# Skip weights loaded as rows, 512-column passes for v and half the output projection, a gelu of four steps, and two gather tiles of one bank

## The chip, the cores and the metric

The kernel runs on one core of a Trainium2 chip. The metric is the device time of one execution in microseconds (us). Before the change three runs gave 1151.94, 1154.35 and 1153.66 us, median 1153.66.

Five engines work side by side and meet at semaphores: TensorE (PE, matmuls; its weight loads are PEld), VectorE (DVE), ScalarE (ACT), GpSimd (POOL) and SyncE (SP, which here only issues DMAs). Sixteen DMA engines move all data for the core.

## What is computed

One layer of a hybrid backbone on 512 latent tokens and 256 context tokens, 1024 channels. After an RMSNorm with modulation comes one wide input projection, and from it two branches: a bidirectional Mamba-2 scan with skip weights per head (d_skip), and a gMLP branch whose halves u and v go through a gelu (v also through a layernorm). Gated, summed and projected by w_o they are added to the input h. Then follows an expert-choice mixture: 16 experts, each takes its best 64 of the 512 tokens.

```python
y = y + d_skip.astype(xh.dtype)[:, None] * xh
u, v = jnp.split(jax.nn.gelu(uv), 2, axis=-1)
sgu = spatial_gating(u, v, n_chunks, ln_w, ln_b, w_s, b_s)
merged = jax.nn.sigmoid(gate_a) * (ssd @ w_pa) + jax.nn.sigmoid(gate_b) * (sgu @ w_pb)
h = h + g1 * (merged @ w_o)
gate, idx = lax.top_k(softmax(xf @ router_w), 64)
hid = silu(xf[idx] @ w_gate) * (xf[idx] @ w_up)
h = h + g2 * scatter(idx, (hid @ w_down) * gate)
```

## The kernel before, in words

All tiles have 128 partitions. The projections of the first half (lines 272 to 965) run each product as three matmuls: an operand is split into a rounded part and its rest (`split`, lines 72 to 78: ACT casts the weights to `wh`, DVE subtracts to get `wl`), and hi times hi, hi times lo and lo times hi are added in one PSUM bank. A scheduler puts the instructions of each engine in an order of its own; on the engine they then run strictly in that order, and each waits for the tiles that it reads and for the readers of the tile that it overwrites. The unit of those waits is the tile, not the part of it that is touched.

**Start (lines 81 to 310).** SP loads x (4 pieces of 512 KB), the first modulation weights `aw`, the first input weights `w0` and the context tokens `ct`, in that order. POOL issues small loads on a queue of its own: rows of parameters, `alog` (one row for all 128 partitions, line 124), `dtb`, and `dsk`, the skip weights (lines 128 to 130): partition 64s+i gets the eight elements s, s+2, s+4, ... The first large matmuls (`gemv`, line 237) wait for `aw`. Then PE transposes x (line 255) and the context (line 261), and ACT copies the results out.

**v (lines 583 to 638).** `token_major` takes the weights in four column blocks of 256. A 1 MB piece of weights is split in two halves, and each half gives 48 matmuls (4 token tiles, 4 rows of k, 3 products) of 256 columns. At the end of a block each token tile goes through `gelu2` (lines 608 to 614: two ACT and three DVE steps) and, every second block, through bn_stats (line 623). The four accumulators `acc` of a block are the only ones, so the next block's first matmul on a token tile waits until its gelu has read the old one out. The steps of the last scan group are laid between (`steps(scans, 2)`). After the last block DVE finishes the layernorm (lines 631 to 636); only then do the pools of this part close, and a load of w_s into the place that they leave (line 751) can go. The u projection (line 770) starts meanwhile.

**Output projection (lines 913 to 965).** The same `token_major` with w_o. A block's token tile goes through `residual` (lines 916 to 921: two DVE steps and one ACT step through the single tile `t0`, so one after the other). `logits` (line 925) transposes two 128-column pieces of h and multiplies by the router's weights, and needs all four token tiles of the block.

**Experts (lines 966 to 1225).** DVE finds the best 64 tokens of each expert (lines 1029 to 1039). The experts go in eight pairs; `project` (line 1089) multiplies the gathered tokens by w_gate and w_up, `down` (line 1154) by w_down, each weight being used once. `piece` (line 687) hands out the 1 MB weight tiles and asks for the next ones: about twenty tiles form a ring, and a load into one waits until PE has read it. The gather of the next pair's tokens is `channels` (line 1074): 16 times 4 matmuls in two halves, each half followed by four ACT steps that scale it into `xg`. Both halves write one PSUM tile of two banks (lines 1106 and 1144). The last pair is cut finer, and the rows go out at line 1238.

Of the kernel before, what the change touches and what calls it, by code (L numbers as in the profile page):

```python
# [7 lines left out]
F32 = mybir.dt.float32  # L8
# [4 lines left out]
AF = mybir.ActivationFunctionType  # L13
OP = mybir.AluOpType
# [3 lines left out]
GELU_C = 0.7978845608028654  # L18
GELU_K = 0.044715

NT = 4
NK = 8
# [11 lines left out]
def tile_backbone(  # L34
# [18 lines left out]
    W = w_in.rearrange("l k n -> (l k) n")  # L53
# [7 lines left out]
    sp = es_s.enter_context(tc.tile_pool(name="sp", bufs=2))  # L61
# [7 lines left out]
    def wtile():  # L69
        return wp.tile([128, 2048], F32, name="w")  # L70
# [5 lines left out]
    def wsplit(hi, lo, src, lo_eng=None):  # L76
        with tc.high_priority():
            split(hi, lo, src, lo_eng)
# [47 lines left out]
    G.memset(dtb, 0.0)  # L126
    nc.gpsimd.dma_start(dtb[0:32, :], dram(dt_bias, 0, [[1, 32], [1, 1]]))
    dsk = sp.tile([128, NK], F32, bufs=1)
    for s in range(2):
        nc.gpsimd.dma_start(dsk[64 * s:64 * s + 64, :], dram(d_skip, s, [[0, 64], [2, NK]]))  # L130

    def rsqrt(o, v, scr, n):

# [30 lines left out]
    def acc():  # L164
        return ps.tile([128, 512], F32, name="acc")
# [4 lines left out]
    with tc.tile_pool(name="st", bufs=2) as st:  # L170
# [81 lines left out]
        for kt in range(NK):  # L252
            p = aux()
# [3 lines left out]
        for k2 in range(NK // 2):  # L257
            p = aux()
# [6 lines left out]
        xmh = xmp.tile([128, NK, 512], F32R, name="xmh")  # L265
        xml = xmp.tile([128, NK, 512], F32R, name="xml")
# [85 lines left out]
    def hl_tile(a, b):  # L352
        return [hl.tile([128, 1024], F32R, name=n)[:, :a * b].rearrange("p (a b) -> p a b", a=a) for n in ("wh", "wl")]
# [8 lines left out]
    def w_cols(src, c0, n):  # L362
        return dram(src, c0, [[src.shape[1], 128], [128 * src.shape[1], NK], [1, n]])
# [7 lines left out]
    for o, n, parts in ((0, 512, (xT,)), (512, 256, (xch.bitcast(F32), xcl.bitcast(F32)))):  # L371
        p = acc()[:, :n]
# [185 lines left out]
    def ahead(gen):  # L558

        cur = next(gen)  # L560
        for n in gen:
            yield cur
            cur = n
        yield cur
# [15 lines left out]
            scans = ssd_group(g)  # L580


    def token_major(src, n0, lh, ll, evac, wt=lambda nb: wtile()):

        def weights():
            for nb in range(4):
                w = wt(nb).rearrange("p (k n) -> p k n", k=NK)
                load(w, w_cols(src, n0 + 256 * nb, 256))
                for kh in range(2):
                    wh, wl = hl_tile(4, 256)  # L590
                    wsplit(wh, wl, w[:, 4 * kh:4 * kh + 4, :])
                    yield nb, kh, wh, wl

        for nb, kh, wh, wl in ahead(weights()):
            if kh == 0:
                pp = [acc()[:, :256] for _ in range(NT)]
            for t in range(NT):
                for k in range(4):
                    kt = 4 * kh + k
                    a = slice(128 * t, 128 * t + 128)  # L600
                    T.matmul(pp[t], lh[:, kt, a], wh[:, k, :], start=kt == 0, stop=False)  # L601
                    T.matmul(pp[t], ll[:, kt, a], wh[:, k, :], start=False, stop=False)  # L602
                    T.matmul(pp[t], lh[:, kt, a], wl[:, k, :], start=False, stop=kt == NK - 1)  # L603
                if kh == 1:
                    evac(nb, t, pp[t])
            yield

    def gelu2(o, p, a):

        S.activation(a, p, AF.Square)  # L610
        V.tensor_scalar(a, a, GELU_C * GELU_K, GELU_C, op0=OP.mult, op1=OP.add)
        V.tensor_mul(a, a, p)
        S.activation(o, a, AF.Tanh)
        V.scalar_tensor_tensor(o, o, 1.0, p, op0=OP.add, op1=OP.mult)  # L614

    vt = big.tile([128, NT, 1024], F32, name="F")
    bn = sp.tile([128, NT, 2, 6], F32, bufs=1)

    def v_out(nb, t, p):
        a = sp.tile([128, 512], F32, name="tm")[:, :256]  # L620
        gelu2(vt[:, t, 256 * nb:256 * nb + 256], p, a)
        if nb % 2:
            V.bn_stats(bn[:, t, nb // 2, :], vt[:, t, 256 * nb - 256:256 * nb + 256])

    for _ in token_major(W, 4128, xmh, xml, v_out):
        steps(scans, 2)
    steps(scans, 99)
    mv = sp.tile([128, NT, 2], F32, bufs=1)
# [51 lines left out]
    def fetch(n):  # L680
        while len(queue) < n:
            w = next(pieces, None)
            if w is None:
                return
            queue.append(w)
# [187 lines left out]
    def half(name, n=512):  # L873
        return rp.tile([128, 512], F32, name=name)[:, :n]
# [38 lines left out]
    h = big.tile([128, NT, 1024], F32, name="F")  # L913
    ssq = rp.tile([128, NT, 4], F32, bufs=1)

    def residual(nb, t, p):
        cs = slice(256 * nb, 256 * nb + 256)
        a = half("t0", 256)
        V.tensor_mul(a, p, g1b[:, cs])
        V.tensor_add(h[:, t, cs], a, x2[:, t, cs])  # L920
        S.activation(a, h[:, t, cs], AF.Square, accum_out=ssq[:, t, nb:nb + 1])

    pl, pt = aux(), aux()

    def logits(nb):

        at = full("m1").rearrange("p (k n) -> p k n", k=2)
        for k in (2 * nb, 2 * nb + 1):
            p = aux()
            for t in range(NT):  # L930
                T.transpose(p[:, 128 * t:128 * t + 128], h[:, t, 128 * k:128 * k + 128], ident)
            if k == NK - 1:
                V.tensor_copy(at[:, k % 2, :], p)
            else:
                S.copy(at[:, k % 2, :], p)
        for k in (2 * nb, 2 * nb + 1):
            if nb == 3:
                for t in range(NT):
                    T.matmul(pt[:, 16 * t:16 * t + 16], at[:, k % 2, 128 * t:128 * t + 128], rwl[:, k % 2, :],
                             start=False, stop=k == NK - 1, skip_group_check=True)  # L940
            else:
                g = slice(32 * (k % 4), 32 * (k % 4) + 32)
                T.matmul(pl[g, :], rw[:, k, :], at[:, k % 2, :], start=nb < 2, stop=k in (2, 3, 4, 5))
        if nb == 2:
            a = half("t0")
            S.copy(a, pl)
            for t in range(NT):
                T.matmul(pt[:, 16 * t:16 * t + 16], a[:, 128 * t:128 * t + 128], sel32[:, 0:16],
                         start=t == 0, stop=False, skip_group_check=True)

    for i, _ in enumerate(token_major(w_o.rearrange("l k n -> (l k) n"), 0, mgh, mgl, residual)):
        if i in {0:11}:
            fetch({0:11}[i])
        if i == 0:
            router_weights()
        elif i == 1:
            router_shift()
            V.tensor_copy(rwl, rw[:, 6:8, 0:16])
            before = half("t1").bitcast(BF)[:, :896]
            steps_ = half("t0").bitcast(I16)[:, :896]  # L960
            G.iota(steps_, pattern=[[1, 896]], base=-384, channel_multiplier=-1)
            V.tensor_scalar(before, steps_, 0.0, -2.0 ** -60, op0=OP.is_le, op1=OP.mult)
        elif i % 2 == 0:
            logits(i // 2 - 1)
    logits(3)
    es_xm.close()
    es_hl.close()
    es_mid.close()
# [102 lines left out]
        S.copy(oh, p)  # L1071
        return oh, gi

    def channels(xt_, ot, hf, p):

        for j in range(4):
            k = 4 * hf + j
            for t in range(NT):
                matmul(p[:, 128 * j:128 * j + 128], x2[:, t, 128 * k:128 * k + 128], ot[:, t, :],
                       start=t == 0, stop=t == NT - 1)  # L1080
        for j in range(4):
            k = 4 * hf + j
            S.activation(xt_[:, k, :], p[:, 128 * j:128 * j + 128], AF.Identity, scale=mcol[:, 8 + k:9 + k],  # L1083
                         bias=mcol[:, k:k + 1])
# [18 lines left out]
    fin = rp.tile([128, 8, NT], F32, name="rst")  # L1103
    q = [fin[:, k, :] for k in range(8)]

    first_banks = pw.tile([128, 2, 512], F32, name="pu", bufs=1)
    for hf in range(2):
        channels(xg, ot, hf, first_banks[:, hf, :])

    def halves_of(hi, lo, c0, a):  # L1110

# [15 lines left out]
    for pr in range(NE // 2):  # L1127
# [13 lines left out]
            xg = tokens()  # L1141
        ht = full("m2").rearrange("p (k n) -> p k n", k=NK)
        if not last:
            gather = pw.tile([128, 2, 512], F32, name="pg", bufs=1)
            channels(xg, ot, 0, gather[:, 0, :])
        for hf in range(2):
            b = gs[hf]
            p = pw.tile([128, 512], F32, name="x")
# [1 line left out]
                transpose(p[:, 128 * k:128 * k + 128], b[:, 128 * k:128 * k + 128], ident)  # L1150
            S.copy(ht[:, 4 * hf:4 * hf + 4, :], p.rearrange("p (k n) -> p k n", k=4))
        if not last:
            channels(xg, ot, 1, gather[:, 1, :])
        def down(c0, c1, nk, behind=None):
            pd = pw.tile([128, 512], F32, name="pd", bufs=2)[:, :c1 - c0]
            for k0 in range(0, NK, nk):
# [112 lines left out]
```

## Time and profile before

| what | before |
|---|---|
| median of 3 runs | 1153.66 us |
| the profiled execution | 1151.37 us |
| its span, first to last instruction | 1149.6 us |
| PE busy | 1070.2 us, 93% of the span |
| DVE busy | 579.2 us, 50% |
| ACT busy | 331.9 us, 29% |
| POOL busy | 66.2 us, 6% |
| DMA engines, mean busy share of the span | 71% |
| bytes moved | 291.85 MB |

Busy time is the time in which an engine had an instruction in work; matmuls are pipelined, so a busy PE need not be at its peak. The chain of waits is followed back from the last instruction, at each step to what released it. The span's 40 slices of 28.7 us show the busy share in tenths. Waits are told in square brackets: idle time, and what ended it.

### The profile page before, as it was taken

The page shows a single profiled execution, that of the slowest core. Times are in us where ns is not written, and L with a number is a line of the kernel's source. Part 1 is how long each engine was busy: PE and PEld are TensorE (multiplying, and loading weights), DVE is VectorE, ACT ScalarE, POOL GpSimd, SP SyncE. Part 2 cuts the span into 40 slices and gives each one's busy share as a digit, 9 for nine tenths or more (in the row PEclk, how much of TensorE's full clock was granted, in tenths as well). Part 3 has the DMA queues.
Part 4 walks back from the last instruction along what each step waited for, and adds up shares of the span by engine and source line. Part 5 has one row for each costly group of instructions (what it writes and reads, how often), then busy time and mean ns, then how long its engine had stood idle before and what let it go on. Part 6 is the DMA issues. An engine that isn't in the chain of part 4 may idle for free.

```text
span 1149.6 us, 15045 instructions
## 1 busy us (share of the span) xinstructions
PE 1070.2 (93%) x5939; PEld 709.5 (62%) x5939; DVE 579.2 (50%) x1061; ACT 331.9 (29%) x645; POOL 66.2 (6%) x58
## 2 busy tenths in 40 slices
PE   2999898999999999999999699999999999999985
PEld 1778777789888888777798545353535353535333
DVE  2768999998698565645653630303030303030305
ACT  4344756554343223323333211010101010101002
POOL 2002231321000000100000000000000000000000
PEclk9999999999999999999999799999999999999998
DMA  9941634231476566622464669999999999999994
GB/s 209 255 132 40 206 101 152 93 87 61 144 263 213 187 221 191 211 86 98 147 259 163 238 238 409 393 408 397 404 401 400 406 395 410 391 409 392 409 393 144
DMA packets 149663, 291.85 MB, mean 254 GB/s; under 512 B 8468, under 2 KB 75188, under 8 KB 149592
## 3 DMA queue, kind: packets, MB, share of 16 engines
q1 hardware_dynamic: 149224, 290.79, 70.5%
q0 software_dynamic: 288, 0.07, 0.7%
q8 instruction: 47, 0.77, 0.3%
q14 instruction: 24, 0.20, 0.1%
q10 hardware_dynamic: 80, 0.02, 0.0%
HBM read 288.67 MB, written 2.18 MB: 253 GB/s over the span
## 4 chain that ended last, share of the span: by engine, by line
PE 74%; DVE 11%; DMA 7%; ACT 4%; issue 3%; POOL 1%; SPq 0%; DVEq 0%; ACTq 0%; POOLq 0%
PE pg L1044 15%; PE pu L1044 10%; PE pd L1044 8%; PE acc L358 7%; PE acc L360 7%; PE acc L359 7%; PE x L1044 4%; PE acc L603 2%; PE acc L601 2%; PE acc L602 2%; DMA w<-in_w_up_dram 2%; DMA aw<-in_ada_w_dram 2%; DVE wl L74 1%; ACT m L1083 1%; DVE gq L515 1%
## 5 line engine op out<-in xcount | busy, mean ns | idle before, releaser
L358 PE MATMUL acc<-xmh,wh 128*128 128x512 f32 x352 | 139.0, 395 | 0.0
L359 PE MATMUL acc<-xml,wh 128*128 128x512 f32 x352 | 138.7, 394 | 0.0
L360 PE MATMUL acc<-xmh,wl 128*128 128x512 f32 x352 | 138.1, 392 | 0.0
L73 ACT CAST wh<-w 128x1024 fp32r<-128x1024 f32 (+1 forms) x84 | 84.4, 1006 | 170.4 <-PE acc L359 133.2
L74 DVE TENSOR_TENSOR wl<-w,wh 128x1024 fp32r<-128x1024 f32 (+1 forms) x81 | 96.3, 1190 | 68.0 <-ACT wh L73 66.8
L1168 DVE SCALAR_TENSOR_TENSOR t<-pd,gi,m 128x512 f32<-128x512 f32 (+2 forms) x17 | 12.2, 719 | 151.6 <-PE pd L1044 137.8
L1123 DVE TENSOR_TENSOR F<-F,x 128x512 f32<-128x512 f32 x56 | 38.5, 687 | 91.3 <-PE x L1044 91.3
L1044 PE MATMUL pg<-e,m 128*64 128x512 f32 x296 | 76.0, 602 | 0.0
L1044 PE MATMUL pu<-e,m 128*64 128x512 f32 x304 | 74.8, 595 | 0.9 <-DMA e<-in_w_up_dram 0.9
L360 PEld LDWEIGHTS acc<-xmh,wl 128*128 128x128 f32 x352 | 66.2, 188 | 14.8 <-issue 1.2
L358 PEld LDWEIGHTS acc<-xmh,wh 128*128 128x128 f32 x352 | 66.2, 188 | 14.6 <-ACT wh L73 0.8
L601 PE MATMUL acc<-wh,xmh 128*128 128x256 f32 x256 | 73.6, 288 | 1.0 <-DVE F L614 1.0
L359 PEld LDWEIGHTS acc<-xml,wh 128*128 128x128 f32 x352 | 66.3, 188 | 13.2 <-issue 0.4
L603 PE MATMUL acc<-wl,xmh 128*128 128x256 f32 x256 | 73.4, 287 | 0.6 <-DVE wl L74 0.6
L602 PE MATMUL acc<-wh,xml 128*128 128x256 f32 x256 | 72.6, 284 | 0.0
L1044 PE MATMUL pd<-e,m 128*64 128x512 f32 x280 | 66.6, 594 | 0.0
L1139 DVE TENSOR_TENSOR t<-t,pu 128x512 f32<-128x512 f32 x16 | 10.3, 683 | 99.6 <-PE pu L1044 99.6
L1083 ACT ACTIVATE m<-pg,mcol 128x128 f32<-128x128 f32 x56 | 21.0, 456 | 135.9 <-PE pg L1044 135.9
L1044 PEld LDWEIGHTS pg<-ot,F 128*128 128x128 f32 x448 | 51.1, 192 | 12.5 <-ACT m L1083 6.8
L1044 PE MATMUL pg<-ot,F 128*128 128x128 f32 x448 | 53.7, 279 | 5.1 <-ACT m L1083 5.1
L358 PE MATMUL acc<-rh,wh 128*128 128x512 f32 x128 | 50.4, 397 | 0.8 <-ACT rh L73 0.5
L603 PEld LDWEIGHTS acc<-wl,xmh 128*128 128x128 f32 x256 | 49.1, 192 | 3.4 <-issue 2.5
(401 smaller groups left out, 1911.8 us busy)
## 6 DMA issues: line engine op xcount, KB each, us to landing
e<-in_w_up_dram SPq DMA_DIRECT2D x38, 1024.0 KB
e<-in_w_gate_dram SPq DMA_DIRECT2D x37, 1024.0 KB
e<-in_w_down_dram SPq DMA_DIRECT2D x35, 1024.0 KB
w<-in_w_in_dram SPq DMA_DIRECT2D x23, 1024.0 KB
f<-in_w_down_dram SPq DMA_DIRECT2D x20, 1024.0 KB
f<-in_w_up_dram SPq DMA_DIRECT2D x19, 1024.0 KB
f<-in_w_gate_dram SPq DMA_DIRECT2D x19, 1024.0 KB
e<-in_ada_w_dram SPq DMA_DIRECT2D x32, 512.0 KB
```

The source lines that it names most:

```text
L73: S.copy(hi, src)
L74: (lo_eng or V).tensor_sub(lo, src, hi.bitcast(F32))
L358: T.matmul(p, wh[:, kt, :], rh[:, kt, :], start=kt == 0, stop=False)
L359: T.matmul(p, wh[:, kt, :], rl[:, kt, :], start=False, stop=False)
L360: T.matmul(p, wl[:, kt, :], rh[:, kt, :], start=False, stop=kt == NK - 1)
L601: T.matmul(pp[t], lh[:, kt, a], wh[:, k, :], start=kt == 0, stop=False)
L602: T.matmul(pp[t], ll[:, kt, a], wh[:, k, :], start=False, stop=False)
L603: T.matmul(pp[t], lh[:, kt, a], wl[:, k, :], start=False, stop=kt == NK - 1)
L1044: return tc.keep_in_program_order(T.matmul(*a, **k))
L1083: S.activation(xt_[:, k, :], p[:, 128 * j:128 * j + 128], AF.Identity, scale=mcol[:, 8 + k:9 + k], bias=mcol[:, k:k + 1])
L1123: V.tensor_add(h[:, t, c0:c0 + 512], h[:, t, c0:c0 + 512], p)
L1168: V.scalar_tensor_tensor(a, pd, gi[:, 0:1], g2k[:, c0:c1], op0=OP.mult, op1=OP.mult)
```

## The change

Five edits. The skip weights are loaded once as a row of 16 for all partitions (`dskr`), and POOL copies each half of the partitions from it with stride 2. `token_major` takes a list of column cuts: v goes in two blocks of 512 columns, w_o in one of 512 and two of 256; a half of a weight piece is then 2 rows of k with 512 columns. `gelu2` loses its first DVE step: the constants go into the other steps. With the wider block `residual` still works in 256 columns, two passes one after the other, and `logits` of the two first blocks come together. The gather takes a tile of one bank for each half, from the two tiles `pd` that `down` and the transposes at line 1023 also use.

```diff
     dsk = sp.tile([128, NK], F32, bufs=1)
+    dskr = sp.tile([128, 2 * NK], F32, bufs=1)
+    nc.gpsimd.dma_start(dskr, row_bc(d_skip, 0, 2 * NK))
     for s in range(2):
-        nc.gpsimd.dma_start(dsk[64 * s:64 * s + 64, :], dram(d_skip, s, [[0, 64], [2, NK]]))
+        g = slice(64 * s, 64 * s + 64)
+        G.tensor_copy(dsk[g, :], dskr[g, :].rearrange("p (k s) -> p s k", s=2)[:, s, :])
...
-            for nb in range(4):
-                w = wt(nb).rearrange("p (k n) -> p k n", k=NK)
-                load(w, w_cols(src, n0 + 256 * nb, 256))
-                for kh in range(2):
-                    wh, wl = hl_tile(4, 256)
-                    wsplit(wh, wl, w[:, 4 * kh:4 * kh + 4, :])
-                    yield nb, kh, wh, wl
+            for c0, c1 in cuts:
+                n = c1 - c0
+                nk, half_ = 2048 // n, 1024 // n
+                for k0 in range(0, NK, half_):
+                    if k0 % nk == 0:
+                        w = wtile().rearrange("p (k n) -> p k n", k=nk)
+                        load(w, dram(src, n0 + c0 + 128 * k0 * src.shape[1],
+                                     [[src.shape[1], 128], [128 * src.shape[1], nk], [1, n]]))
+                    wh, wl = hl_tile(half_, n)
+                    wsplit(wh, wl, w[:, k0 % nk:k0 % nk + half_, :])
+                    yield c0, c1, k0, half_, wh, wl
...
         S.activation(a, p, AF.Square)
-        V.tensor_scalar(a, a, GELU_C * GELU_K, GELU_C, op0=OP.mult, op1=OP.add)
-        V.tensor_mul(a, a, p)
-        S.activation(o, a, AF.Tanh)
+        V.scalar_tensor_tensor(a, a, 1.0 / GELU_K, p, op0=OP.add, op1=OP.mult)
+        S.activation(o, a, AF.Tanh, scale=GELU_C * GELU_K)
         V.scalar_tensor_tensor(o, o, 1.0, p, op0=OP.add, op1=OP.mult)
...
-    for _ in token_major(W, 4128, xmh, xml, v_out):
+    for _ in token_major(W, 4128, xmh, xml, v_out, ((0, 512), (512, 1024))):
...
+    def residual(c0, c1, t, p):
+        for c in range(c0, c1, 256):
+            nb, cs, ps_ = c // 256, slice(c, c + 256), slice(c - c0, c - c0 + 256)
...
+                                        ((0, 512), (512, 768), (768, 1024)))):
...
-    def channels(xt_, ot, hf, p):
+    def channels(xt_, ot, hf):
+        p = pw.tile([128, 512], F32, name="pd", bufs=2)
...
-    first_banks = pw.tile([128, 2, 512], F32, name="pu", bufs=1)
     for hf in range(2):
-        channels(xg, ot, hf, first_banks[:, hf, :])
+        channels(xg, ot, hf)
...
-            gather = pw.tile([128, 2, 512], F32, name="pg", bufs=1)
-            channels(xg, ot, 0, gather[:, 0, :])
+            channels(xg, ot, 0)
...
-            channels(xg, ot, 1, gather[:, 1, :])
+            channels(xg, ot, 1)
```

The order of the instructions moves at three places of which the prediction speaks. A row is a line of the program, an operation, output<-inputs and the output's shape. The lines of the changed kernel are a few higher than those of the kernel before.

First, POOL's queue at the start. Before:

```order
L124 DMA alog<-in_a_log_dram 128x32
L126 MEMSET dtb 128x1
L130 DMA dsk<-in_d_skip_dram 64x8x1
L127 DMA dtb<-in_dt_bias_dram 32x1
L130 DMA dsk<-in_d_skip_dram 64x8x1
L74 TENSOR_TENSOR wl<-w,wh 128x1024
```

And in the change:

```order
L124 DMA alog<-in_a_log_dram 128x32
L126 MEMSET dtb 128x1
L130 DMA dskr<-in_d_skip_dram 128x16
L127 DMA dtb<-in_dt_bias_dram 32x1
L133 COPY dsk<-dskr 64x8 x2
L74 TENSOR_TENSOR wl<-w,wh 128x1024
```

Two loads by single elements have become one load of a row of 16, in the same place, and two copies on POOL that wait for it; behind them POOL has nothing until the weight split of the first scan groups.

Second, DVE where the gelu of the first v block stands among the scan's steps (L611 to L614 are gelu2, L515, L519, L527 and L535 the scan, L74 is wl). Before:

```order
L515 SCALAR_TENSOR_TENSOR gq<-cb_2485,dt,gq 128x128
L612 TENSOR_TENSOR tm<-tm,acc 128x256
L74 TENSOR_TENSOR wl<-w,wh 128x1024
L614 SCALAR_TENSOR_TENSOR F<-F,acc 128x256 x2
L611 TENSOR_SCALAR tm<-tm 128x256
L515 SCALAR_TENSOR_TENSOR gq<-cb_2485,dt,gq 128x128
L612 TENSOR_TENSOR tm<-tm,acc 128x256
```

And in the change, where L619 and L621 are gelu2 and L518, L522, L530 and L538 the scan:

```order
L518 SCALAR_TENSOR_TENSOR gq<-cb_2415,dt,gq 128x128 x8
L522 TENSOR_TENSOR seg<-seg,gq 128x1024
L74 TENSOR_TENSOR wl<-w,wh 128x1024
L530 SCALAR_TENSOR_TENSOR F<-F,dsk,aux 128x512
L538 TENSOR_TENSOR E_2200<-E_2200,aux 128x512
L538 TENSOR_TENSOR E_2203<-E_2203,aux 128x512
L619 SCALAR_TENSOR_TENSOR tm<-tm,acc 128x512
L621 SCALAR_TENSOR_TENSOR F<-F,acc 128x512
L619 SCALAR_TENSOR_TENSOR tm<-tm,acc 128x512
```

The gelu no longer stands between the scan's steps: it comes after nearly all of them, in one stretch, with twice the columns.

Third, PE and ACT at the end of the first block of w_o. Before, on PE (L931 are the transposes of `logits`, eight at a time):

```order
L601 MATMUL acc<-wh,xmh 128x256
L602 MATMUL acc<-wh,xml 128x256
L603 MATMUL acc<-wl,xmh 128x256
L931 MATMUL aux<-ident,F 128x128 x8
L601 MATMUL acc<-wh,xmh 128x256
```

In the change, on PE, behind the first twelve matmuls of the second block, which are its first token tile and stand right behind the last matmul of 512 columns (L937 are the transposes; four here, and two and two later):

```order
L609 MATMUL acc<-wh,xmh 128x256
L610 MATMUL acc<-wh,xml 128x256
L611 MATMUL acc<-wl,xmh 128x256
L937 MATMUL aux<-ident,F 128x128 x4
L609 MATMUL acc<-wh,xmh 128x256
```

and on ACT, beside it (L927 is the last step of a residual pass, L73 the cast of the next weights, L941 copies transposes out):

```order
L927 ACTIVATE t_4887,ssq<-F 128x256
L927 ACTIVATE t_4891,ssq<-F 128x256
L73 CAST wh<-w 128x1024
L927 ACTIVATE t_4901,ssq<-F 128x256
L927 ACTIVATE t_4905,ssq<-F 128x256
L927 ACTIVATE t_4915,ssq<-F 128x256
L927 ACTIVATE t_4919,ssq<-F 128x256
L927 ACTIVATE t_4929,ssq<-F 128x256
L941 COPY m_4993<-aux 128x512 x2
```

Eight residual passes now follow one another at one block's end, with a cast between the second and the third, while PE's second block, which needs their accumulators, stands right behind the first.

## Rows read from the trace of the kernel before

**Rows 1.** The page's slices of 28.7 us: DMA share in tenths, and bytes moved.

```profile
DMA  9941634231476566622464669999999999999994
GB/s 209 255 132 40 206 101 152 93 87 61 144 263 213 187 221 191 211 86 98 147 259 163 238 238 409 393 408 397 404 401 400 406 395 410 391 409 392 409 393 144
```

**Rows 2.** Stretches of the start: length, busy us (x instructions) by engine, PEclk, DMA share, GB/s.

```profile
5.00:10.00 5.00, 0.29 (x1) 0.18 (x1) 0.46 (x3) 3.84 (x7) 1.95 (x4) 1.00 1.14 346
10.00:15.00 5.00, 0.00 (x0) 0.00 (x0) 3.26 (x17) 2.50 (x5) 0.00 (x0) 1.00 1.07 80
```

**Rows 3.** DMA queues from 9 to 21 us, then from 4 to 10 us (last line): packets, MB, share.

```profile
q0 software_dynamic: 97, 0.00, 63.5%
q1 hardware_dynamic: 1887, 1.23, 34.3%
...
q0 software_dynamic: 195, 0.06, 15.0%
```

**Rows 4.** Issues on POOL's queue, which is q0: KB, us to landing.

```profile
dsk<-in_d_skip_dram POOLq DMA_DIRECT2D x2, 2.0 KB, 12.3
alog<-in_a_log_dram POOLq DMA_DIRECT2D x1, 16.0 KB, 5.0
```

**Rows 5.** Chain of waits at the start: start us, us, what.

```profile
4.45 17.64 DMA aw<-in_ada_w_dram
22.22 1.97 PE aux L237 x16
32.11 2.10 PE aux L261 x16
```

**Rows 6.** Timeline of ACT at the start: start us, us.

```profile
12.33 2.19 ACT L226 ACTIVATE F<-F,rr 128x1024 f32<-128x1024 f32 x2 [2.02 <-DVE rr L143]
```

**Rows 7.** Stretches from v to the experts; columns as in rows 2.

```profile
306.00:590.00 284.00, 279.63 (x1293) 224.90 (x1292) 180.12 (x217) 92.78 (x125) 6.88 (x5) 1.00 0.55 178
660.00:670.00 10.00, 8.36 (x61) 6.20 (x61) 9.35 (x18) 3.00 (x8) 0.00 (x0) 0.99 0.01 3
```

**Rows 8.** Timeline of PE: two 256-column matmuls 45 apart, two of 512 42 apart.

```profile
236.06 0.28 PE L603 MATMUL acc<-wl,xmh 128*128 128x256 f32 x1
241.45 0.28 PE L603 MATMUL acc<-wl,xmh 128*128 128x256 f32 x1
296.21 0.40 PE L358 MATMUL acc<-xmh,wh 128*128 128x512 f32 x1
305.75 0.39 PE L358 MATMUL acc<-xmh,wh 128*128 128x512 f32 x1
```

**Rows 9.** Groups of lines, 235 to 309 us: busy us, mean ns, idle before.

```profile
L611 DVE TENSOR_SCALAR tm<-tm 128x256 f32<-128x256 f32 x16 | 5.6, 349 | 0.2
L527 DVE SCALAR_TENSOR_TENSOR F<-F,dsk,aux 128x512 f32<-128x512 f32 x3 | 2.2, 742 | 0.9 <-PE aux L526 0.9
```

**Rows 10.** Chain of waits around the end of v.

```profile
308.91 4.28 DMA e<-in_w_s_dram
```

**Rows 11.** Timeline of PE around the end of v, with waits.

```profile
313.54 0.63 PE L760 MATMUL aux<-ident,e 128*128 128x128 f32 x4 [1.51 <-DMA e<-in_w_s_dram]
```

**Rows 12.** Timeline of DVE and ACT in the output projection.

```profile
637.12 0.42 DVE L919 TENSOR_TENSOR t<-acc,m 128x256 f32<-128x256 f32 x1 [0.66 <-ACT t L921]
638.64 0.42 DVE L919 TENSOR_TENSOR t<-acc,m 128x256 f32<-128x256 f32 x1 [0.64 <-ACT t L921]
...
588.88 1.05 ACT L73 CAST wh<-w 128x1024 fp32r<-128x1024 f32 x1 [3.61 <-PE acc L602]
```

**Rows 13.** Timeline of PE at the first gather and at one inside the loop.

```profile
663.33 3.84 PE L1044 MATMUL pu<-ot,F 128*128 128x128 f32 x32 [1.64 <-ACT m L1083]
...
702.27 3.84 PE L1044 MATMUL pg<-ot,F 128*128 128x128 f32 x32 [0.78 <-ACT m L1083]
```

**Rows 14.** DMA from 672 to 1112 us.

```profile
DMA packets 59970, 176.33 MB, mean 401 GB/s; under 512 B 2679, under 2 KB 2679, under 8 KB 59949
```

**Rows 15.** Chain of waits in the last pair.

```profile
1087.81 18.45 DMA w<-in_w_up_dram
```

More of the change, by code (lines that the diff above doesn't have):

```diff
@@ L580, in tile_backbone, with token_major @@
             scans = ssd_group(g)
-    def token_major(src, n0, lh, ll, evac, wt=lambda nb: wtile()):
+    def token_major(src, n0, lh, ll, evac, cuts):
         def weights():
-            for nb in range(4):
-                w = wt(nb).rearrange("p (k n) -> p k n", k=NK)
-                load(w, w_cols(src, n0 + 256 * nb, 256))
-                for kh in range(2):
-                    wh, wl = hl_tile(4, 256)
-                    wsplit(wh, wl, w[:, 4 * kh:4 * kh + 4, :])
-                    yield nb, kh, wh, wl
-        for nb, kh, wh, wl in ahead(weights()):
-            if kh == 0:
-                pp = [acc()[:, :256] for _ in range(NT)]
+            for c0, c1 in cuts:
[9 more added lines that the diff above has]
+                    yield c0, c1, k0, half_, wh, wl
+        for c0, c1, k0, nk, wh, wl in ahead(weights()):
+            if k0 == 0:
+                pp = [acc()[:, :c1 - c0] for _ in range(NT)]
             for t in range(NT):
-                for k in range(4):
-                    kt = 4 * kh + k
+                for k in range(nk):
+                    kt = k0 + k
                     a = slice(128 * t, 128 * t + 128)
@@ L603, in token_major @@
                     T.matmul(pp[t], lh[:, kt, a], wl[:, k, :], start=False, stop=kt == NK - 1)
-                if kh == 1:
-                    evac(nb, t, pp[t])
-            yield
+                if k0 + nk == NK:
+                    evac(c0, c1, t, pp[t])
+            yield c1 if k0 + nk == NK else None
     def gelu2(o, p, a):
         S.activation(a, p, AF.Square)
-        V.tensor_scalar(a, a, GELU_C * GELU_K, GELU_C, op0=OP.mult, op1=OP.add)
-        V.tensor_mul(a, a, p)
-        S.activation(o, a, AF.Tanh)
+        V.scalar_tensor_tensor(a, a, 1.0 / GELU_K, p, op0=OP.add, op1=OP.mult)
+        S.activation(o, a, AF.Tanh, scale=GELU_C * GELU_K)
         V.scalar_tensor_tensor(o, o, 1.0, p, op0=OP.add, op1=OP.mult)
@@ L617, in tile_backbone, with v_out @@
     bn = sp.tile([128, NT, 2, 6], F32, bufs=1)
[L619 to L623, printed above, removed]
-    for _ in token_major(W, 4128, xmh, xml, v_out):
+    def v_out(c0, c1, t, p):
+        gelu2(vt[:, t, c0:c1], p, sp.tile([128, 512], F32, name="tm"))
+        V.bn_stats(bn[:, t, c0 // 512, :], vt[:, t, c0:c1])
+    for _ in token_major(W, 4128, xmh, xml, v_out, ((0, 512), (512, 1024))):
         steps(scans, 2)
@@ L914, in tile_backbone @@
     ssq = rp.tile([128, NT, 4], F32, bufs=1)
[L916 to L921, printed above, removed]
+    def residual(c0, c1, t, p):
+        for c in range(c0, c1, 256):
+            nb, cs, ps_ = c // 256, slice(c, c + 256), slice(c - c0, c - c0 + 256)
+            a = half("t0", 256)
+            V.tensor_mul(a, p[:, ps_], g1b[:, cs])
+            V.tensor_add(h[:, t, cs], a, x2[:, t, cs])
+            S.activation(a, h[:, t, cs], AF.Square, accum_out=ssq[:, t, nb:nb + 1])
     pl, pt = aux(), aux()
@@ L949, in logits @@
                          start=t == 0, stop=False, skip_group_check=True)
-    for i, _ in enumerate(token_major(w_o.rearrange("l k n -> (l k) n"), 0, mgh, mgl, residual)):
-        if i in {0:11}:
-            fetch({0:11}[i])
+    done = 0
+    for i, end in enumerate(token_major(w_o.rearrange("l k n -> (l k) n"), 0, mgh, mgl, residual,
+                                        ((0, 512), (512, 768), (768, 1024)))):
         if i == 0:
+            fetch(11)
             router_weights()
@@ L962, in tile_backbone @@
             V.tensor_scalar(before, steps_, 0.0, -2.0 ** -60, op0=OP.is_le, op1=OP.mult)
-        elif i % 2 == 0:
-            logits(i // 2 - 1)
-    logits(3)
+        elif i > 3:
+            while done < ready_:
+                logits(done)
+                done += 1
+        ready_ = end // 256 if end else done
+    while done < 4:
+        logits(done)
+        done += 1
     es_xm.close()
```

## The prediction

> **What bounds the kernel now.** I read the views in the order of the groups: slices of the span, queues and chain at the start, then stretches, then single rows at the places that the change touches. The bound is another one in each of three parts.
>
> *Start, to about 32 us.* The chain begins with the load of `aw`, which lands at 4.45 + 17.64 = 22.09, and PE's first gemv matmuls start at 22.22 [rows 5]. Yet the DMA engines move little: the rate is 346 GB/s from 5 to 10 us and 80 from 10 to 15, at a busy share of 1.07 [rows 2]. Engines that are busy and move nothing are held by something small. From 9 to 21 us POOL's queue has 63.5% of all sixteen engines' time with 97 packets and no MB to speak of, while SP's queue moves its 1.23 MB in 34.3% [rows 3]. On POOL's queue stand the two loads of `dsk`, 2 KB each and 12.3 us to landing [rows 4]: 64 partitions times 8 single elements each.
>
> *v to the mixture.* From 306 to 590 us PE is busy 279.63 of 284 us [rows 7]: PE's own work sets the time, and what it has done earlier at 306 is kept.
>
> *Experts.* From 660 to 670 us the engines stand at a share of 0.01 [rows 7]: the ring is full and waits for PE. From 672 to 1112 they move 176.33 MB at 401 GB/s [rows 14], the highest level of the page [rows 1], and in the last pair PE still waits 18.45 us for a weight [rows 15]. This stretch is a transfer of fixed length. What is won before 671 moves it forward as a whole; what PE saves within it becomes a longer wait for weights.
>
> **The change part by part.** The sum is made against the profiled execution, 1151.37 us with a span of 1149.6; the runs' median, 1153.66, is 2.3 above it. A measurement of this kernel can tell about 0.2%, 2.3 us, from no change.
>
> *A, skip weights.* Removed: 1024 single elements. Added: 128 rows of 64 bytes, and two POOL copies of 64x8 that nobody needs before the scans. The nearest row is `alog`, 128 rows of 128 bytes, 5.0 us to landing [rows 4]; it lies among the 195 packets of 4 to 10 us that took only 15.0% of the engines, 0.9 us [rows 3]. So the hold goes. What SP's queue moved from 9 to 21 us, 1.23 MB, takes 3.6 us at 346 GB/s; that puts `aw` at 12.6 at the latest, and as some of it belongs to the loads behind `aw` I take 12.0: 22.1 − 12.0 = **−10.1**. The next limit is close: x is scaled by ACT until 12.33 + 2.19 = 14.52 [rows 6], and its transposes stand on PE behind the first gemv (1.97 us [rows 5]) and its reading out, so at about 15. From there everything keeps its distance, the context's transposes (32.11 now [rows 5]) starting at about 22. Bounds: −11 (`aw` one us sooner still); −7.3, if the hold lasts as long as a row load takes to land, 5.0 in place of 12.3 us.
>
> The Trainium skill (page "DMA: Bandwidth & Descriptors", section "Specifications") speaks against this edit: it asks for at least 512 bytes per transfer for the full rate, and a row of 64 is below that as much as a single element is. By it alone the new load would be as slow as the old, and A nothing. The row of `alog`, also far below 512 bytes, disagrees: 5.0 us, not 12.3 [rows 4].
>
> *B, v in 512 columns and the shorter gelu.* A 256-column matmul costs (241.45 − 236.06)/45 = 0.120 us, one of 512 (305.75 − 296.21)/42 = 0.227 [rows 8]. v has 384 of 256, 46.1 us; 192 of 512 are 43.6: −2.5 on PE. DVE loses sixteen steps of 349 ns, 5.6 us, and the others become half as many, at the 742 ns of the scan's step of 512 columns [rows 9]. That lies beside PE. What counts is the end of the part: PE stands at L760, 313.54, after 1.51 us of waiting for w_s [rows 11], whose load, 4.28 us, starts at 308.91 when the layernorm is done [rows 10]. That tail hardly moves (I take 0.4 us earlier), so v's saving would become a longer wait, were it not that the new order puts 87 matmuls of u ahead of L760 where there were 69: 18 × 0.227 = 4.1 us of u done in the same time. With the 0.4 that is 4.5; I take **−4.0**, as two full banks per block end may cost PE a wait. Bounds: −0.4 (only the tail) and −5 (PE's saving, its wait here and one more us).
>
> *C, half of w_o in 512 columns.* On PE 192 × 0.120 = 23.0 becomes 96 × 0.227 = 21.8: −1.25. But at the first block's end eight residual passes run one after the other, 638.64 − 637.12 = 1.52 us each, as each waits for ACT to release `t0`; and ACT has a cast of 1.05 us between them [rows 12]. A bank is free after its second pass, so one in 3.04 us, while PE comes with a token tile of the second block each 12 × 0.120 = 1.44 us and some transposes. Followed tile by tile, PE waits about 0.9, 1.6 and 1.3, so +3.8. Sum **+2.6**; bounds −1.25 (transposes and second halves fill the gaps) and +5.
>
> *D, the first gather.* Before the second half's matmuls at 663.33 PE waits 1.64 us for ACT to read the first half, as both lie in one tile [rows 13]. With two tiles this goes: **−1.6**. It stands before 671, so it counts. Bounds −1.6 and 0, if the ring's first slot is freed by something else.
>
> *E, the gathers inside the loop.* Seven of 0.78 [rows 13], 5.5 us in all. They lie in the saturated stretch: **0**; the cover is the DMA, and without it they are worth −5.5. `pd` is now shared with `down`, and PE might wait for a bank there; under the same cover.
>
> Sum: −10.1 − 4.0 + 2.6 − 1.6 = −13.1, so 1138.3 against the profiled execution and **1140.6** on the level of the runs.
>
> **Rivals.** *The hold shrinks, but not to nothing.* A at its bound of −7.3: 1143.4. For it: the new load still has 128 pieces; against: `alog`'s had as many.
>
> *The gathers in the loop count.* If the 401 GB/s are not the limit but what a waiting ring gives, E brings 5.5: 1135.1. For it: the chain passes PE's lines too. Against: the share stays at the page's highest, and the 18.45 us at the end.
>
> *The change does not do what it says at the start*: the row load holds the engines as the single elements do, A is 0, and 1150.7 results, just at the edge of no change. The skill's size rule above would make it so.
>
> *Full banks (slower).* There are four accumulators. With 512 columns all four are full at a block's end, and if PE finds nothing else to do it waits for the whole reading out. In the middle of v that is, per token tile, two DVE steps of 0.74 [rows 9] and two ACT steps of about half a 1.05 cast [rows 12], 2.5 us, 10 for four; in w_o eight passes and two casts, 8 × 1.52 + 2.1 = 14.3 [rows 12]. These 24.3 in place of the 3.8 in my sum give 1161. It decides from when the waits pass 3.8 + 13.1 + 2.3 = 19.2 us. For it: the gelu now stands in one stretch behind the scan's steps on DVE. Against: in PE's order both halves of a token tile and the transposes are laid between, and in v the scans' matmuls.
>
> **How the numbers follow.** Forecast 0.62; smaller gain at the start 0.12; loop gathers 0.10; no gain at the start 0.09; full banks 0.07. The forecast's own bounds, mostly C and B, are about 3 us down and 6 up. The range, **1133.5 to 1149**, takes in the first three cases and leaves out the last two and a tail. Faster by over 0.2%: the first three and half of the fourth, 0.89. Within 0.2%: the other half, 0.05. Slower: 0.06.
>
> **What would show it.** A: `aw` lands near 12, the first gemv starts there, and the slow stretch of 10 to 20 us is gone; an `aw` later than 15 makes A wrong. B: L760 about 14 us earlier than 313.54; if only 10, B is wrong. C: PE's waits at the first w_o block's end near 3.8; over 8 it is the bank rival. D: no wait before the first gather's second half. E: the DMA still near 401 GB/s for 440 us, its start moved by the sum, and PE's wait in the last pair longer by about 5; if that wait shrinks and the end comes sooner, E was wrong.

## The result and the profile after

| what | before | after |
|---|---|---|
| median of the runs | 1154.01 us (4 runs) | 1137.37 us (1132.59 to 1138.49, 4 runs) |
| the profiled execution, its span | 1151.37, 1149.6 us | 1138.34, 1136.6 us |
| PE busy | 1070.2 us, 93% | 1072.8 us, 94% |
| DVE busy | 579.2 us | 570.0 us |
| PE's mean granted clock | 0.989 | 0.985 |

The ratio is 0.9851, 95% interval 0.9819 to 0.9883: 17 us faster, 14 to 21. The kernel was run again beside the experiments (`change_again` below): 1134.98 against 1152.01, ratio 0.986 [0.9842, 0.9878]; before that run 0.988 was expected if the parts add up as they stand alone and 0.985 if they help each other. Forecast were 1140.6 us in a range of 1133.5 to 1149, and faster with 0.89.

The page's slices of the change, to set beside [rows 1]. The slice to see is the first: 290 GB/s where 209 stood.

```profile
DMA  9832524232566675623373699999999999999993
GB/s 290 233 80 89 176 92 165 76 111 75 189 207 217 200 259 171 192 87 119 138 283 109 241 339 409 390 409 392 407 398 404 402 398 407 394 409 392 409 389 121
```

The first stretches of the change (columns as in [rows 2]), then its DMA queues from 9 to 21 us, then its chain of waits (start us, us, what):

```profile
5.00:10.00 5.00, 0.30 (x1) 0.18 (x1) 0.46 (x3) 4.07 (x9) 1.03 (x3) 1.00 1.02 297
10.00:15.00 5.00, 1.88 (x16) 0.68 (x16) 3.33 (x17) 2.90 (x5) 0.37 (x2) 1.00 1.10 371
15.00:20.00 5.00, 4.46 (x25) 4.41 (x22) 1.98 (x5) 3.28 (x7) 0.00 (x0) 1.00 1.11 321
```

```profile
q1 hardware_dynamic: 5832, 3.94, 105.2%
q0 software_dynamic: 80, 0.01, 0.5%
```

```profile
4.44 8.55 DMA aw<-in_ada_w_dram
...
13.12 1.97 PE aux L240 x16
```

From 10 to 15 us 371 GB/s move where 80 did, POOL's queue takes 0.5% of the engines where it took 63.5% [rows 3], and `aw` lands at 12.99 where it landed at 22.09 [rows 5].

To follow the gain through the program, the same instruction is looked up on PE's and SP's timelines in three profiles: before, after, and `change_again`. Each cell is its start in us; in brackets how much earlier it is than before.

| instruction | before | after | change_again |
|---|---|---|---|
| first gemv | 22.22 | 13.12 (9.1) | 13.62 (8.6) |
| context transposes | 32.10 | 23.00 (9.1) | 23.49 (8.6) |
| last scan matmul (L534) before v | 233.93 | 228.29 (5.6) | 224.41 (9.5) |
| first matmul on the half that follows w_s | 356.95 | 346.25 (10.7) | 344.66 (12.3) |
| first matmul of w_o | 582.99 | 572.30 (10.7) | 570.13 (12.9) |
| last transposes of `logits` | 641.09 | 629.11 (12.0) | 626.93 (14.2) |
| first `project` | 667.10 | 652.27 (14.8) | 650.68 (16.4) |
| weight stream starts again (SP) | 670.78 | 655.95 (14.8) | 654.36 (16.4) |
| rows go out (SP) | 1141.02 | 1127.93 (13.1) | 1125.00 (16.0) |

The two profiles of the same kernel differ in three places: before v after lost 3.5 us that `change_again` kept, and at the end 1.3; behind v `change_again` lost 1.6 that after kept. All three are stretches in which PE was granted half its clock; a section below shows them.

### The profile page after: what moved, and what is told of

The parts are those of the page before. It is cut to its first block, busy times and chain, and to the rows that moved or that the text cites. A ratio compares the mean times of both kernels' runs of the same rounds, so it can differ in the third digit from the quotient of the medians.

```text
span 1136.6 us, 14388 instructions
## 1 busy us (share of the span) xinstructions
PE 1072.8 (94%) x5651; PEld 698.4 (61%) x5651; DVE 570.0 (50%) x1021; ACT 329.6 (29%) x629; POOL 66.2 (6%) x59
## 4 chain that ended last, share of the span: by engine, by line
PE 75%; DMA 10%; DVE 10%; issue 2%; ACT 2%; SPq 1%; POOL 1%; DVEq 0%; ACTq 0%; POOLq 0%
PE pd L1056 12%; PE pg L1056 9%; PE pu L1056 8%; PE acc L361 8%; PE acc L363 7%; PE acc L362 7%; PE x L1056 3%; PE acc L611 2%; PE acc L610 2%; PE acc L609 2%; DMA e<-in_w_gate_dram 2%; DMA e<-in_w_up_dram 2%; DMA f<-in_w_down_dram 1%; DMA w<-in_w_gate_dram 1%; PE aux L537 1%
## 5 line engine op out<-in xcount | busy, mean ns | idle before, releaser
L73 ACT CAST wh<-w 128x1024 fp32r<-128x1024 f32 (+1 forms) x84 | 84.4, 1006 | 178.9 <-PE acc L362 126.5
L74 DVE TENSOR_TENSOR wl<-w,wh 128x1024 fp32r<-128x1024 f32 (+1 forms) x81 | 96.1, 1187 | 71.1 <-ACT wh L73 70.6
L362 PEld LDWEIGHTS acc<-xml,wh 128*128 128x128 f32 x352 | 66.4, 189 | 12.9
L1096 ACT ACTIVATE m<-pd,mcol 128x128 f32<-128x128 f32 x64 | 24.1, 458 | 147.3 <-PE pd L1056 147.3
L1056 PEld LDWEIGHTS pd<-ot,F 128*128 128x128 f32 x512 | 59.4, 195 | 5.9 <-issue 5.9
L1056 PE MATMUL pd<-ot,F 128*128 128x128 f32 x512 | 61.5, 279 | 0.0
L609 PE MATMUL acc<-wh,xmh 128*128 128x512 f32 (+1 forms) x160 | 56.5, 354 | 0.0
L611 PE MATMUL acc<-wl,xmh 128*128 128x512 f32 (+1 forms) x160 | 56.1, 351 | 0.1
L610 PE MATMUL acc<-wh,xml 128*128 128x512 f32 (+1 forms) x160 | 56.1, 351 | 0.0
L1056 PEld LDWEIGHTS pu<-e,m 128*64 128x64 f32 x304 | 26.2, 137 | 44.6 <-issue 36.8
```

The costliest lines, as they stand in the source:

```text
L73: S.copy(hi, src)
L74: (lo_eng or V).tensor_sub(lo, src, hi.bitcast(F32))
L362: T.matmul(p, wh[:, kt, :], rl[:, kt, :], start=False, stop=False)
L1056: return tc.keep_in_program_order(T.matmul(*a, **k))
```

## The experiments

Eleven kernels. Each was timed in turns with the kernel before on the same chip; a ratio stands with its 95% interval. Parts put into the kernel before show what one is worth alone, parts taken out of the change what is missing without it. The diffs are cut to the lines that tell; the kernel before is there written with its four blocks as a list of cuts.

**The skip weights alone, and the change without them.** `only_skip` is the kernel before with this edit alone; `undo_skip` is the change with it reversed:

```diff
-    dskr = sp.tile([128, 2 * NK], F32, bufs=1)
-    nc.gpsimd.dma_start(dskr, row_bc(d_skip, 0, 2 * NK))
     for s in range(2):
-        g = slice(64 * s, 64 * s + 64)
-        G.tensor_copy(dsk[g, :], dskr[g, :].rearrange("p (k s) -> p s k", s=2)[:, s, :])
+        nc.gpsimd.dma_start(dsk[64 * s:64 * s + 64, :], dram(d_skip, s, [[0, 64], [2, NK]]))
```

> The kernel before with the skip weights as one row, and nothing else. If the single elements held the DMA engines (theory), aw lands near 13.0 in place of 22.1 and the first gemv starts at 13.1; the time falls by 9 if all of it is kept, by 5.6 if PE's clock falls between 95 and 130 us again as in the profile of the change (its shift there went from -9.1 to -5.6). If that clock loss is not tied to the earlier start, the shift at 145 us is near -9. Rival (something else in the change made the early start): aw lands near 22 and the time stays within 2 us.

> The change with the two loads by single elements put back. Theory: aw lands near 22.1, and what is left of the gain is v, w_o and the gather, by the shifts between the two profiles 5.1 + 1.3 + 2.8 less 1.8 given back at the end, so 6 to 9 us below before. If the parts share their gain, it is 11 or more.

Measured: `only_skip` 1143.22 against 1151.2, 0.9929 [0.9915, 0.9944], 8.2 us; `undo_skip` 1145.53, 0.9951 [0.9937, 0.9965], 5.6 us, a little under the 6 to 9 expected (its interval is 4.0 to 7.3). The start goes with this edit alone. In the chains of waits `aw` lands with it at 13.35 (`only_skip`) and without it at 22.11 (`undo_skip`, whose first gemv starts at 22.24 as before):

```profile
4.51 8.84 DMA aw<-in_ada_w_dram
...
13.49 1.97 PE aux L240 x16
```

```profile
4.49 17.62 DMA aw<-in_ada_w_dram
...
22.24 1.97 PE aux L237 x16
```

**Twice the single elements.** `dose_double` is the change with 2048 single elements in place of the row:

```diff
-    nc.gpsimd.dma_start(dskr, row_bc(d_skip, 0, 2 * NK))
+    for s in range(2):
+        nc.gpsimd.dma_start(dskr[:, NK * s:NK * s + NK], dram(d_skip, s, [[0, 128], [2, NK]]))
     for s in range(2):
         g = slice(64 * s, 64 * s + 64)
-        G.tensor_copy(dsk[g, :], dskr[g, :].rearrange("p (k s) -> p s k", s=2)[:, s, :])
+        G.tensor_copy(dsk[g, :], dskr[g, NK * s:NK * s + NK])
```

> The change with 2048 single elements on POOL's queue in place of the row load (twice those of before). If the hold goes with the number of single elements, POOL's queue takes about twice its 7.6 us of all sixteen engines, the landing of aw moves from 13.0 to 31 (9.1 per 1024 elements), and the time is some 18 above the change. If one load of any such kind costs a fixed time, aw lands at about 22 and the time is as undo_skip's, 1145.

Measured: 1154.08, 1.0038 [1.0022, 1.0055], 19 us above the change on the same chip. Its chain of waits:

```profile
4.36 27.52 DMA aw<-in_ada_w_dram
...
32.01 1.97 PE aux L241 x16
```

POOL's queue from 4 to 40 us (packets, MB, share of 16 engines), first of `dose_double`, then of before, then of the change:

```profile
q0 software_dynamic: 288, 0.07, 48.6%
```

```profile
q0 software_dynamic: 288, 0.07, 22.6%
```

```profile
q0 software_dynamic: 256, 0.07, 3.7%
```

With none, 1024 and 2048 single elements of the skip weights it is (in the order change, before, `dose_double`) 3.7, 22.6 and 48.6% of 36 us, and `aw` at 13.0, 22.1 and 31.9. The number of rows does not do it: the change loads 128 rows as before does, nor the bytes, 8 KB in the change and 4 before. So 1024 elements, 4 KB in all, kept all sixteen engines for 7 to 9 us and put `aw` off by 9 to 10. The Trainium skill says why they were single (page "DMA: Bandwidth & Descriptors", section "Rules for kernel authors"): a strided last dimension is lowered to one descriptor per element. The queue's share, which grows with the elements, goes with that; its packets, 288 for 1024 as for 2048, do not show the single descriptors. The size rule of that page's section "Specifications", which asks for 512 bytes per transfer, would have had the row of 64 bytes as slow: the 3.7% above, in which the row load is contained, speak against that reading for so few rows.

**w_o alone.**

```diff
-                                        ((0, 256), (256, 512), (512, 768), (768, 1024)))):
+                                        ((0, 512), (512, 768), (768, 1024)))):
...
```

> The kernel before with the first half of w_o in 512 columns only. The prediction's sum had +2.6 (PE waiting 3.8 for accumulators); the profile of the change shows no wait of PE there and a shift of -1.3. So theory now: -1.3, with no PE wait between 600 and 640. The rival, waits at the block's end, gives +2.6.

Measured: 1150.07, 0.9993 [0.9982, 1.0004]: 0.8 us, between 2.1 faster and 0.5 slower. The +2.6 lie outside. In the table, from the first matmul of w_o to the last transposes of `logits`, the change takes 56.81 us (`change_again` 56.80) and the kernel before 58.10: −1.3, the pace alone, and no wait for a bank; `only_wo`'s own profile takes 56.76. DVE and PE of the change at the end of the first block show why. DVE reads the second half of the second, third and fourth bank:

```profile
597.34 0.42 DVE L925 TENSOR_TENSOR t<-acc,m 128x256 f32<-128x256 f32 x1
600.38 0.42 DVE L925 TENSOR_TENSOR t<-acc,m 128x256 f32<-128x256 f32 x1 [0.64 <-ACT t L927]
603.41 0.42 DVE L925 TENSOR_TENSOR t<-acc,m 128x256 f32<-128x256 f32 x1 [0.64 <-ACT t L927]
```

PE's timeline, the first matmul of the block, and where, by the order of its instructions, the third and the fourth token tile begin (the second of each two):

```profile
595.14 0.28 PE L609 MATMUL acc<-wh,xmh 128*128 128x256 f32 x1
...
600.79 0.51 PE L609 MATMUL acc<-wh,xmh 128*128 128x256 f32 x2
...
603.71 0.63 PE L609 MATMUL acc<-wh,xmh 128*128 128x256 f32 x2
```

A bank is free at 600.80 and the next at 603.83. PE comes to them at about 600.9 and 603.8. In the order of its instructions the second half of an earlier tile lies between: from the start of the second tile to that of the third it has 22 matmuls and two transposes, from the third to the fourth 21 and two, 2.9 us, where the prediction counted 12 matmuls. So PE and the banks nearly tie. The pairs above take 0.51 and 0.63 us where two matmuls take 0.40 (0.12 + 0.28); so at most 0.1 and 0.2 us are lost, and the profile lists no wait.

**The gather alone, and the change without it.** `only_gather` puts the two bank tiles into the kernel before, `undo_gather` takes them out of the change (its diff, and read backwards that of `only_gather`):

```diff
+    first_banks = pw.tile([128, 2, 512], F32, name="pu", bufs=1)
...
-        channels(xg, ot, hf)
+        channels(xg, ot, hf, first_banks[:, hf, :])
...
-            channels(xg, ot, 0)
+            gather = pw.tile([128, 2, 512], F32, name="pg", bufs=1)
+            channels(xg, ot, 0, gather[:, 0, :])
...
-            channels(xg, ot, 1)
+            channels(xg, ot, 1, gather[:, 1, :])
```

> The kernel before with the two bank tiles of the gather only. The prediction: the wait of 1.64 before the first gather's second half goes, -1.6, and nothing from the loop; the profiles show -2.85 at the first gather, of which 1.2 is a clock that rises sooner. If the loop's seven waits of 0.78 counted it would be -7. The shift within 672 to 1112 us tells these apart: constant by the first, growing by 0.8 a pair by the second.

> The change with the gather's two halves in one tile again. Alone the two tiles gave nothing (0.9995): so theory says this kernel equals the change within 2 us. The first gather's second half waits 1.6 again, the restart of the weight stream comes 1.6 later, and the loss is taken back at the end; rival: with the wait the time is 1.6 to 3 above the change.

Measured: `only_gather` 1151.14, 0.9995 [0.9984, 1.0006]; `undo_gather` 1137.03, 0.9878 [0.9861, 0.9896], 2 us above `change_again`, with intervals that overlap. The times are too coarse for 1.6 us. The timeline of PE is not. First `change_again`, then `undo_gather`:

```profile
641.74 9.01 PE L1056 MATMUL pd<-ot,F 128*128 128x128 f32 x64
650.68 1.51 PE L1056 MATMUL pg<-e,m 128*64 128x512 f32 x6
```

```profile
639.83 5.00 PE L1056 MATMUL pu<-ot,F 128*128 128x128 f32 x32
646.47 3.84 PE L1056 MATMUL pu<-ot,F 128*128 128x128 f32 x32 [1.64 <-ACT m L1095]
650.24 1.08 PE L1056 MATMUL pg<-e,m 128*64 128x512 f32 x4
```

From the first gather matmul to the first `project` it is 8.94 us with two tiles, 10.41 with one. In all profiles of this study: 8.35 to 9.66 with two (six kernels), 10.37 to 11.23 with one (six), and 13.45 in `only_wo`, where PE had half its clock longer. The wait of 1.64 [rows 13] is gone, about what was forecast. In the loop the seven waits of 0.7 to 0.8 go too (5.1 us in the waits of `only_skip`, none in `only_gather`), and nothing comes of it: from the restart of the weight stream to the rows that go out it is 470.24 us before, 470.62 in `undo_gather`, 470.64 in `change_again`, and 469.99 to 470.64 in eleven of the thirteen profiles. The two others, after and `only_gather`, have 472.0 and 472.1; in both PE was at half its clock some 20 us before that end. (`only_wo` had this 37 us before it, while PE was waiting for weights anyway, and kept 469.99.)

**v: both edits, the columns alone, the gelu alone.**

```diff
-    for _ in token_major(W, 4128, xmh, xml, v_out, ((0, 256), (256, 512), (512, 768), (768, 1024))):
+    for _ in token_major(W, 4128, xmh, xml, v_out, ((0, 512), (512, 1024))):
```

```diff
-        V.tensor_scalar(a, a, GELU_C * GELU_K, GELU_C, op0=OP.mult, op1=OP.add)
-        V.tensor_mul(a, a, p)
-        S.activation(o, a, AF.Tanh)
+        V.scalar_tensor_tensor(a, a, 1.0 / GELU_K, p, op0=OP.add, op1=OP.mult)
+        S.activation(o, a, AF.Tanh, scale=GELU_C * GELU_K)
```

> The kernel before with v in 512 columns and the shorter gelu only. Prediction: -4.0; the profiles of before and change say -5.1 between the start of v and the part behind w_s. If the gain belongs to the start only (rival), it is within 2 us of before.

> The kernel before with v in two blocks of 512 columns and the old gelu. By PE's pace alone (192 x 0.227 for 384 x 0.120) it brings -2.5, and with what the new order lays ahead of w_s up to -4; only_v with both gave -3.8. If the columns are what counts, -3 to -4 here; if the shorter gelu is, about 0.

> The kernel before with the shorter gelu alone, v in 256 columns. It takes 349 ns from each of 16 DVE steps in v and those of u beside a busy PE, so theory says within 1 us of before; the rival (DVE sets the end of v) says -2 or more.

Measured: `only_v` 1148.17 against 1152.01, 0.9967 [0.9951, 0.9983], 3.8 us. `v_cuts` 1151.38 against 1152.37, 0.9989 [0.9978, 0.9999], 1.3 us; `gelu_only` 1151.1, 0.9992 [0.9982, 1.0001], 0.9 us. What I expected of the columns alone (3 to 4) was wrong as a time (its interval is 0.1 to 2.5), yet right for the stretch. From the last scan matmul before v to the half that follows w_s it is 123.02 us before, 117.72 in `only_v`, 119.10 in `v_cuts` and 122.17 in `gelu_only`: −5.3, −3.9 and −0.9. `v_cuts` then gives most of it back. Some 10 us further on PE waits in `v_cuts` for the splits of DVE and ACT, as it does neither before nor in `only_v`:

```profile
365.34 0.50 PE L359 MATMUL acc<-rl,wh 128*128 128x512 f32 x1 [0.59 <-DVE rl L74]
...
367.14 0.50 PE L358 MATMUL acc<-xmh,wh 128*128 128x512 f32 x1 [0.60 <-ACT wh L73]
```

Its lead over before is 3.7 us at the half behind w_s and 1.9 from 373 us on, and a stretch at half clock near 474 takes nearly all the rest. `only_v` differs from `v_cuts` by the gelu alone; there the waits are absent, and a lead of 5.9 at the same half is still there at w_o. So the columns bring PE onto work of DVE and ACT that is as long as before, and the shorter gelu, worth little alone, seems to let the lead stand. One profile each shows that; in time the two intervals, 2.0 to 5.6 and 0.1 to 2.5 us, still overlap.

**The last dip.** From 8.5 to 9.25 us the rate of the change is still only 27 to 44 GB/s. `late_small` loads dtb and the skip weights' row on SP's queue:

```diff
-    nc.gpsimd.dma_start(dtb[0:32, :], dram(dt_bias, 0, [[1, 32], [1, 1]]))
...
-    nc.gpsimd.dma_start(dskr, row_bc(d_skip, 0, 2 * NK))
...
             load(ct[:, t * 1024:(t + 1) * 1024], cr[t * 128:(t + 1) * 128, :])
+        load(dtb[0:32, :], dram(dt_bias, 0, [[1, 32], [1, 1]]))
+        load(dskr, row_bc(d_skip, 0, 2 * NK))
...
```

> The change, with the loads of dtb (32 single elements) and of the row of skip weights moved from POOL's queue to SP's, behind aw and the context. In the profile of the change the rate still falls to 27 to 40 GB/s for about 1.3 us before 10 us, while POOL's queue has 38% of the engines. If those two loads hold them, aw lands 1 us sooner, near 12, as the prediction had it, and the time is 1 below the change, no more, as x is scaled only at 14.3. If the dip is something else, nothing moves.

Measured: 1136.11 against 1152.37, 0.9858 [0.9844, 0.9872], the change's 0.986. The dip is shallower (123 to 181 GB/s in the same stretch), so the two loads made part of it. Its first gemv starts at 12.93, and not for `aw` any more:

```profile
12.93 1.94 PE L240 MATMUL aux<-aw,scp 128*32 128x256 f32 x16 [5.19 <-DVE F L231]
```

L231 is DVE's scaling of x. The start is now bound by x nearly as much as by `aw`: against the gemv at 13.12 and 13.62 of the change's two profiles an `aw` at 12.0, as forecast, would have brought 0.2 to 0.7 us. No kernel here is clearly faster than the change.

## Why the prediction was right

The predicted 1140.6 lies 3.2 us above the measured median. That it is so near is in part luck, as A came out smaller than forecast and C better. By its own terms, with the shifts of `change_again`, whose clock was the least disturbed of the two (one fall, inside B):

| term | predicted | measured |
|---|---|---|
| A, skip weights | −10.1 | −8.6 at the gemv, −9.5 before v; alone −8.2 in time |
| B, v and gelu | −4.0 | −2.8 to the half behind w_s (−5.1 in after), −3.3 to w_o; −5.3 in `only_v`'s profile, −3.8 in its time |
| C, half of w_o | +2.6 | −1.3; alone −0.8 in time |
| D, first gather | −1.6 | −2.3, of which some is PE's clock |
| E, gathers in the loop | 0 | +0.4 |
| sum | −13.1 | −16.0 in the profiles, −16.1 [−18.2, −14.1] and −17.2 [−20.9, −13.5] in time |

The two times are the ratios of `change_again` and of the first measurement, times their medians of before, 1152.01 and 1154.01. The parts alone add up to 13.4 us (8.2, 3.8, 0.8 and 0.6 for the gathers), and the change without the skip edit keeps 5.6 of 16.1. That the parts help each other is not shown: the intervals leave room for a plain sum.

**A was right** in mechanism and place. The hold is the single elements', by dose; it goes whole, and the two rivals at the start (part of it stays, all of it stays) are out. The term was 0.6 to 1.5 too large: `aw` landed at 12.99 and 13.35 (after, `only_skip`), not at 12.0, and near that a second limit stands: in `change_again` and `late_small` the gemv's last wait is for DVE's scaling of x, one step sooner in the chain than the prediction put this limit.

**B was right** in mechanism and size, but its sign was not. The 18 matmuls of u that the order puts ahead of w_s, priced at 4.1 us, are seen between L765 (L760 before) and the half behind w_s: 43.41 us before, 39.28 in after, and 39.23 to 39.28 in all seven profiles with the wide v and an undisturbed clock there. In `change_again` it is 40.86, as PE's clock fell at 304 us; this explains most of the gap between its −2.8 and the −5.1 of after. The rest of B is the tail, 0.2 to 0.9 shorter where 0.4 was forecast. L765 in after and in `change_again`:

```profile
306.97 0.63 PE L765 MATMUL aux<-ident,e 128*128 128x128 f32 x4 [1.08 <-DMA e<-in_w_s_dram]
```

```profile
303.80 1.00 PE L765 MATMUL aux<-ident,e 128*128 128x128 f32 x4 [1.90 <-DMA e<-in_b_s_dram]
```

This is 6.6 and 9.7 us earlier than 313.54. The prediction wanted 14 and called B wrong at 10, against its own sum: with a tail that hardly moves, this place can come earlier by A alone, and B's gain shows behind it. The prediction also priced the two edits together and put the gelu beside PE at nothing; alone the columns keep 1.3 of the 3.8 us.

**C failed**, and is most of the difference to the measured time: 3.9 us. The step that failed is "PE comes with a token tile of the second block each 12 × 0.120 = 1.44 us". The order lays the second half of an earlier tile between, so PE comes each 2.9 us, and a bank is free each 3.04. The prediction names this very order as its point against the rival of full banks, yet left it out of the term. The lower bound of the term, −1.25, is what was measured. The rival of full banks rested on the same step and is out: the change's profile lists no wait of PE for a bank at the three ends of a wide block.

**D and E were right.** D's wait is gone in six profiles. E's waits are gone too, and the stream takes as long as before; from 657 to 1097 us of the change:

```profile
DMA packets 59923, 176.24 MB, mean 401 GB/s; under 512 B 2678, under 2 KB 2678, under 8 KB 59902
```

The same 401 GB/s as in [rows 14]. One reading behind it was wrong: the 18.45 us of [rows 15] are the time of a transfer, not of a wait. PE's waits for weights in the last pair before are these, 3.9 us:

```profile
1101.18 3.22 PE L1044 MATMUL pu<-e,m 128*64 128x512 f32 x13 [0.91 <-DMA e<-in_w_up_dram]
...
1106.30 3.65 PE L1044 MATMUL pu<-w,m 128*64 128x512 f32 x14 [1.47 <-DMA w<-in_w_up_dram]
...
1118.51 3.65 PE L1162 MATMUL pd<-f,m 128*64 128x512 f32 x16 [1.57 <-DMA f<-in_w_down_dram]
```

The sign named for E, a wait in the last pair longer by 5, did not come: in `change_again` that wait is 3.4 us, and 2.4 more lie in the seventh pair. The sum grows by 1.9 only, while 5.1 us of waits at the gathers went; PE's busy time in the stretch grows by 3.1, from 455.27 to 458.38 us, and why stays open. What decides for E is the length of the stretch, 470.24 and 470.64 us. The chain of the change names transfers in the seventh and the last pair (start us, us, what):

```profile
979.24 13.80 DMA w<-in_w_gate_dram
...
1010.41 18.50 DMA e<-in_w_up_dram
...
1052.53 19.67 DMA e<-in_w_gate_dram
...
1087.95 15.58 DMA f<-in_w_down_dram
```

## What to carry to other kernels

Where the DMA engines are busy and move nothing, look for a small transfer behind it: the one with the fewest bytes per piece; load it as a row, and take it apart on an engine that has nothing to do. Where an engine sets the pace, an edit beside it may be worth little alone and may still decide whether another one keeps its gain. Before a wait for a bank is priced, read in the order what the waiting engine does until it gets there, over all halves of the work and not the next one alone.

## What the hardware showed that was not expected

PE's granted clock falls from 2.4 to 1.2 GHz for some 3 to 4 us, at one place in seven profiles and at others in a few. The rows show that place, just behind the first matmul of dA (L409 before), in the kernel after, in `change_again` and before.

In the kernel after (columns as in [rows 2], the third number from the end is the granted clock, 0.50 being 1.2 GHz):

```profile
99.00:101.00 2.00, 1.58 (x9) 1.58 (x10) 0.79 (x3) 0.42 (x1) 0.00 (x0) 0.76 1.14 327
101.00:103.00 2.00, 2.00 (x7) 1.46 (x7) 0.65 (x2) 0.55 (x2) 0.24 (x1) 0.50 0.52 130
```

In `change_again`, at the same place of the program:

```profile
101.00:103.00 2.00, 2.00 (x17) 1.74 (x16) 1.11 (x3) 0.57 (x3) 0.47 (x1) 1.00 0.85 213
```

Before:

```profile
110.00:112.00 2.00, 2.00 (x18) 1.79 (x17) 1.52 (x4) 1.09 (x3) 0.97 (x1) 1.00 0.53 132
```

Ahead of it PE waited 1.7 us for DVE in all three. After's lead over before shrinks there from 9.0 to 7.3 us, by the same matmuls on the two timelines. Seven of the thirteen profiles have this fall, six have not, with and without each edit, so it isn't the change's. The change's profile has a second one 24 to 28 us behind it and a third in the last pair; together they are the 3.5 and 1.3 us named above. `change_again` has its own, behind the 1.90 us for which PE waits at L765:

```profile
304.00:306.00 2.00, 2.00 (x8) 1.71 (x7) 0.00 (x0) 0.58 (x1) 0.00 (x0) 0.50 1.02 412
```

Such falls explain part of the 6 us between the fastest and the slowest run of the change; that they explain all of it was not tried. What decides whether one comes stays open.
